# A decoder block on eight cores: prep transfers tied to their moment by semaphores, norm work moved to the front, x loads spread, one weight cast later, elementwise work for two engines

## The chip, the cores and the metric

The kernel runs on one Trainium2 chip, on 8 cores at once. Each core handles one sequence of 4096 tokens, and no core talks to another. The metric is device time in microseconds (us) of the slowest core, lower is better. Some executions fall into a slower state in which the cores of one die (0 to 3 or 4 to 7) or of both are granted a lower TensorE clock. "Fast" below means a run outside that state.

## The reference, cut to what matters

One layer with three sub-layers, each with a conditioned RMSNorm in front, and a final norm:

```python
h = ada_rmsnorm(x, g_ffn1, sh1, sc1)
x = x + 0.5 * gt1 * swiglu_ffn(h, w_ffn1_in, w_ffn1_out)      # d_ff = 2816
h = ada_rmsnorm(x, g_mix, sh2, sc2)
proj = h @ w_in                                                # 1024 -> 2048
y_conv = conformer_conv_group(...)                             # 31-wide conv, LayerNorm, silu
y_rnn  = rglru_group(...)                                      # conv4, gates, linear recurrence
x = x + gt2 * (concat([y_conv, y_rnn]) @ w_out)
h = ada_rmsnorm(x, g_ffn2, sh3, sc3)
x = x + 0.5 * gt3 * swiglu_ffn(h, w_ffn2_in, w_ffn2_out)
return ada_rmsnorm(x, g_final, f_shift, f_scale)
```

Width 1024, float32 in and out. The shifts, scales and gates (`sh1` and so on) come from a small matrix product of the conditioning vector.

## The kernel before

The kernel is written as a list of operations for five queues: PE (TensorE), ACT (ScalarE), DVE (VectorE), SP (SyncE, which issues DMAs) and PL (GpSimd, which issues DMAs that convert float32 to bf16). On the host a list scheduler simulates them and fixes the order of each queue. At any simulated moment, an engine takes the ready operation with the lowest priority number. What the scheduler decides is only an order. At run time the engines are held to each other by semaphores, and only where data or a buffer demands it:

```python
def emit(eng, fn, reads=(), writes=(), dma=None):
    ...
    for r in reads:
        need(r.w)                      # wait for the writer
    for w in writes:
        need(w.w)                      # wait for the last writer and the readers
        ...
```

An operation can also be told to come `after` another. In this kernel that matters to the scheduler alone. No semaphore carries it.

The sequence is cut into 8 tiles of 512 tokens. The first FFN runs over pairs of tiles (4 pairs). The mixer and the second FFN run tile by tile. In the first pair the weights of the first FFN are cast while they are loaded, and written back to DRAM as bf16. All other weights are cast by 54 "prep" transfers, DRAM to DRAM, on GpSimd's queue, each placed `after` a matmul of the pairs 2 to 4:

```python
prep = [(nm, r) for nm in ("win", "dcw", "wout", "w2i", "w2o") for r in range(len(scr[nm]))]
...
for n, (nm, r) in enumerate(prep):
    a = mid[min(len(mid) - 1, n * len(mid) * 9 // (len(prep) * 10))]
    dma("PL", lambda d=d: d.ap, lambda src=src: src, 3 << 19, lambda n=n: psems[n % 8],
        [], [d, psem[n % 8]], after=(a,), prio=450 + n)
```

The norm is a sum of squares (ScalarE squares, TensorE sums over partitions with a matrix of ones), a reciprocal root on ScalarE, then a product on VectorE and a shift on ScalarE, whose bf16 output feeds the matmuls:

```python
def norm(xs, msc, msh, after=()):
    r = stats(xs, after)                       # 8 squares, 8 ones-matmuls, Ln, Exp
    for f in range(8):
        stt(t_, xs[f], gs[msc][:, f], r, ALU.mult, ALU.mult, ...)      # VectorE  (cut)
        act(b, t_, AF.Identity, bias=modv[msh][:, f], ...)             # ScalarE  (cut)
...
for pi, tiles in enumerate(pairs):
    P.prio = 500 + pi * 100
    ...
    hbs = [norm(xs, M_SC1, M_SH1, after=(last_in,)) for xs in xss]
...
def mix_ffn2(t):
    P.prio = 1000 + 10 * t
    ...
    hb = norm(xs, M_SC2, M_SH2)
    ...                                        # mixer of tile t
    P.prio = 1100 + 10 * t
    hb2 = norm(xs, M_SC3, M_SH3)
    ...                                        # second FFN of tile t
```

## Time and profile before

| | before |
|---|---|
| time, median of 3 runs | 2750.63 us |
| TensorE busy | 2403.1 of 2746.4 us |
| TensorE waits for the first FFN's weight slabs | 124.5 us, 3 waits |
| TensorE waits for ScalarE's bf16 outputs (`sb_h`) | 124.1 us, 31 waits |

The page of the kernel before, parts 1 and 2 (busy us, share of the span, instructions; then busy tenths in 40 equal slices of about 69 us, TensorE's granted clock in tenths, and the busy share of the DMA engines):

```profile
PE 2403.1 (87%) x11179; PEld 1121.6 (41%) x11392; DVE 985.2 (36%) x1632; ACT 982.6 (36%) x1538; POOL 114.5 (4%) x221
PE   1999829984799689978998998998999999989796
PEclk9999969997899899989999999999999999999998
DMA  9998894589646964534464554554545545545442
```

TensorE is nearly full except at the start and in three hollows (slices 5 to 6, 9 to 10 and 14), where the DMA line reads 8 or 9.

The table of who waited for whom, TensorE's four largest rows (us in total, times, longest):

```profile
PE ps L418 <- DMA sb_slab<-b_w1i: 124.5, 3, 54.4
PE ps L418 <- ACT sb_h L390: 124.1, 31, 16.2
PE ps L418 <- DVE sb_c L394: 35.4, 7, 10.1
PE ps L418 <- ACT sb_c L390: 23.5, 15, 2.0
```

The timeline of DMA issues around the first hollow, first from GpSimd's queue, then from SyncE's (start, us, queue, out<-in, count):

```profile
297.95 3.91 POOL L425 DMA_DIRECT2D b_win<-win  x8
308.72 0.49 POOL L425 DMA_DIRECT2D b_dcw<-dcw  x1 [6.86 <-DMA b_win<-win]
...
347.85 0.49 POOL L425 DMA_DIRECT2D b_wout<-wout  x1 [4.80 <-DMA b_dcw<-dcw]
...
531.10 0.51 POOL L425 DMA_DIRECT2D b_wout<-wout  x1
```

```profile
306.34 81.47 SPq L425 DMA_DIRECT2D sb_c<-x  x16
387.90 1.19 SPq L425 DMA_DIRECT2D sb_slab<-b_w1i  x2
```

Seventeen prep transfers leave in 50 us, then none of them for 183 us, until the next residual stores unblock the queue. In the middle of the burst SyncE needs 81 us to issue 16 loads of x, and the weight slab for which TensorE waits is the next in its queue. The chain of waits shows that two of the 16 issues take 65 of these 81 us, and what follows (start, us, what):

```profile
315.30 16.83 SPq L425
...
332.94 48.54 SPq L425
...
387.90 11.60 DMA sb_slab<-b_w1i
...
400.55 12.67 PE ps L418 x49
...
413.28 10.74 PE ps L418 x49
```

The first piece of 49 matmuls after the stall takes 12.67 us, later ones 10.74.

In the second half of the kernel there are no large holes, but small ones in every tile. TensorE's timeline in one tile of the mixer stage (start, us, operation, out<-in, shapes, count, and in brackets the idle time before and what ended it):

```profile
2042.93 0.38 PE L418 MATMUL ps<-sb_h,sb_ones 128*128 128x512 bf16 x1
2044.69 1.91 PE L418 MATMUL ps<-sb_ub,sb_slab 128*128 128x256 bf16 x16 [1.38 <-ACT sb_c L390]
2048.62 5.30 PE L418 MATMUL ps<-sb_h,sb_slab 128*128 128x512 bf16 x16 [2.02 <-ACT sb_c L390]
...
2071.00 0.38 PE L418 MATMUL ps<-sb_h,sb_ones 128*128 128x512 bf16 x1
2075.60 4.85 PE L418 MATMUL ps<-sb_h,sb_slab 128*128 128x512 bf16 x11 [4.22 <-DVE sb_c L394]
```

Waits of 1.4, 2.0 and 4.2 us.

### The profile page before, as it was taken

To read this page: it belongs to the slowest core of one execution; us is meant where nothing else is said; L and a number is where in the kernel's file an instruction comes from. 1 tells how busy PE (TensorE), PEld (TensorE's weight loads), DVE (VectorE), ACT (ScalarE), POOL (GpSimd) and SP (SyncE) were. 2 spreads that over 40 slices of the span, in tenths; PEclk is the share of its full clock that TensorE was granted. 3 is DMA by queue.
4 is the path that set the end of the run, shared out by engine and by line. 5 is a ranking of instruction groups with operands and counts; after the bars stand their busy time and mean duration, and the time that the engine had idled before them with its cause. 6 is when DMAs were issued, how large, how long until landed. Compare 5 with 4: busy or idle time off the path is not lost.

```text
span 2746.4 us, 34315 instructions; the slowest of 8 cores (2738.7 to 2746.4 us)
## 1 busy us (share of the span) xinstructions
PE 2403.1 (87%) x11179; PEld 1121.6 (41%) x11392; DVE 985.2 (36%) x1632; ACT 982.6 (36%) x1538; POOL 114.5 (4%) x221
## 2 busy tenths in 40 slices
PE   1999829984799689978998998998999999989796
PEld 0444304432344234444444444444454444444343
DVE  4321303231232323266326345255154263362211
ACT  3211201220120311176337338257266274373312
POOL 0001100010001100100000000000000000000000
PEclk9999969997899899989999999999999999999998
DMA  9998894589646964534464554554545545545442
GB/s 264 190 244 219 136 193 143 146 181 115 214 138 177 135 191 157 191 123 154 123 184 145 181 180 146 179 190 161 192 155 168 183 161 166 180 145 184 154 142 73
DMA packets 130365, 460.32 MB, mean 168 GB/s; under 512 B 16048, under 2 KB 16176, under 8 KB 129328
## 3 DMA queue, kind: packets, MB, share of 16 engines
q1 hardware_dynamic: 113184, 378.15, 42.9%
q0 software_dynamic: 17008, 79.97, 16.8%
q8 instruction: 96, 1.57, 0.2%
q14 instruction: 77, 0.63, 0.1%
HBM read 453.07 MB, written 79.69 MB: 194 GB/s over the span
## 4 chain that ended last, share of the span: by engine, by line
PE 78%; ACT 6%; SPq 6%; DMA 4%; issue 3%; DVE 2%; POOL 0%; DVEq 0%; ACTq 0%; POOLq 0%
PE ps L418 78%; SPq L425 6%; ACT sb_c L390 4%; DMA sb_slab<-b_w1i 3%; ACT sb_h L390 1%; DVE sb_c L394 1%; DMA sb_slab<-wmod 1%; ACT L390 1%; DVE sb_c L398 0%; DMA sb_c<-xmid 0%; DVE sb_slab L474 0%; DVE sb_h L408 0%; POOL y L425 0%; DVEq L111 0%; ACTq L111 0%
## 5 line engine op out<-in xcount | busy, mean ns | idle before, releaser
L418 PE MATMUL ps<-sb_h,sb_slab 128*128 128x512 bf16 x9783 | 2206.8, 385 | 255.5 <-DMA sb_slab<-b_w1i 124.5
L418 PEld LDWEIGHTS ps<-sb_h,sb_slab 128*128 128x128 bf16 x9984 | 985.9, 99 | 1457.8 <-issue 317.3
L390 ACT ACTIVATE sb_c<-ps 128x512 f32<-128x512 f32 x400 | 237.0, 596 | 1076.1 <-PE ps L418 1053.6
L398 DVE TENSOR_TENSOR sb_h<-ps,sb_c 128x512 bf16<-128x512 f32 x352 | 242.8, 691 | 942.5 <-PE ps L418 863.3
L390 ACT ACTIVATE sb_h<-sb_c 128x512 bf16<-128x512 f32 x288 | 172.7, 624 | 337.6 <-DVE sb_c L394 198.8
L394 DVE SCALAR_TENSOR_TENSOR sb_c<-ps,sb_gth,sb_c 128x512 f32<-128x512 f32 x128 | 95.4, 749 | 416.2 <-PE ps L418 412.6
L390 ACT ACT_TABLE_LOAD x95 | 121.9, 1283 | 252.4 <-PE ps L418 246.8
L394 DVE SCALAR_TENSOR_TENSOR sb_c<-sb_c,sb_gs 128x512 f32<-128x512 f32 x256 | 173.2, 745 | 62.7 <-ACT sb_c L390 62.7
L418 PE MATMUL ps<-sb_h,sb_ones 128*128 128x512 bf16 x309 | 98.0, 393 | 57.4 <-ACT sb_h L390 53.5
L474 DVE SCALAR_TENSOR_TENSOR sb_slab<-sb_slab,sb_crow 128x1024 f32<-128x1024 f32 x88 | 107.1, 1217 | 83.0 <-DMA sb_slab<-wmod 81.8
L390 ACT ACTIVATE sb_h<-sb_c,sb_modv 128x512 bf16<-128x512 f32 x192 | 126.4, 716 | 20.9 <-DVE sb_c L394 11.4
L418 PE MATMUL ps<-sb_ub,sb_slab 128*128 128x256 bf16 x1024 | 116.1, 273 | 9.5 <-ACT sb_c L390 9.4
L418 PEld LDWEIGHTS ps<-sb_ub,sb_slab 128*128 128x128 bf16 x1024 | 99.1, 98 | 29.7 <-issue 16.6
L425 POOL DMA_DIRECT2D y<-sb_c x64 | 34.4, 540 | 1542.4 <-ACT sb_c L390 1538.9
L398 DVE TENSOR_TENSOR sb_c<-sb_c 128x512 f32<-128x512 f32 x96 | 61.8, 684 | 42.7 <-ACT sb_c L390 42.7
L394 DVE SCALAR_TENSOR_TENSOR sb_c<-ps,sb_modv,sb_c 128x512 f32<-128x512 f32 x64 | 48.0, 751 | 76.2 <-PE ps L418 70.4
L418 PEld LDWEIGHTS ps<-sb_h,sb_ones 128*128 128x128 bf16 x320 | 31.3, 98 | 104.7 <-issue 77.1
L394 DVE SCALAR_TENSOR_TENSOR sb_c<-sb_ux,sb_vecs,sb_c 128x512 f32<-128x512 f32 x96 | 69.5, 745 | 1.7
L425 POOL DMA_DIRECT2D xmid<-sb_c x64 | 34.8, 544 | 762.0 <-DVE sb_c L394 755.6
L390 ACT ACTIVATE sb_c<-ps,sb_vecs 64x256 f32<-64x256 f32 x128 | 60.3, 484 | 14.9 <-PE ps L418 12.4
L394 DVE SCALAR_TENSOR_TENSOR sb_ub<-sb_c,ps 64x256 bf16<-64x256 f32 x128 | 53.8, 420 | 15.0 <-PE ps L418 11.5
L390 ACT ACTIVATE sb_c<-sb_c,sb_lam 128x512 f32<-128x512 f32 x64 | 49.3, 818 | 0.0
(47 smaller groups left out, 472.1 us busy)
## 6 DMA issues: line engine op xcount, KB each, us to landing
sb_slab<-b_w2i SPq DMA_DIRECT2D x176, 512.0 KB, 3.8
sb_slab<-b_w2o SPq DMA_DIRECT2D x96, 512.0 KB, 3.8
sb_slab<-wmod SPq DMA_DIRECT2D x88, 512.0 KB, 6.9
sb_slab<-b_w1i SPq DMA_DIRECT2D x66, 512.0 KB, 5.3
sb_slab<-b_win SPq DMA_DIRECT2D x64, 512.0 KB, 4.3
sb_slab<-b_dcw SPq DMA_DIRECT2D x64, 512.0 KB, 3.6
sb_slab<-b_w1o SPq DMA_DIRECT2D x36, 512.0 KB, 4.5
sb_c<-x SPq DMA_DIRECT2D x64, 256.0 KB, 26.1
```

The costliest lines, as they stand in the source:

```text
L390: return A("ACT", dur, lambda: (lambda o, i: (lambda h: [h.activation(out=o, in_=i, func=func, bias=bias, scale=scale)]))(out(), in_()), r ...
L394: return A("DVE", dur, lambda: (lambda o, a, b: (lambda h: [h.scalar_tensor_tensor(out=o, in0=a, scalar=scalar, in1=b, op0=op0, op1=op1)]) ...
L398: return A("DVE", dur, lambda: (lambda o, a, b: (lambda h: [h.tensor_tensor(out=o, in0=a, in1=b, op=op)]))(out(), in0(), in1()), reads, wr ...
L418: return [h.matmul(o, lhsT=l, rhs=r, start=(first and i == 0), stop=(last and i == n - 1)) for i, (l, r) in enumerate(pr)]
L425: lambda: (lambda o, i: (lambda h: [h.dma_start(out=o, in_=i)]))(out(), in_()),
L474: return lambda h: [h.scalar_tensor_tensor(out=w, in0=w, scalar=1.0, in1=crow.ap, op0=ALU.mult, op1=ALU.mult, accum_out=o)]
```

## The change

Its intent is to use DMA time evenly and to keep TensorE supplied. The diff, cut to its core (the scheduler's handling of an operation that may run on either of two engines, and formatting, are left out; so is one small edit: the loads of the modulation weights, `wmod`, no longer come `after` a step, only the products that use them do):

```diff
-def emit(eng, fn, reads=(), writes=(), dma=None):
+def emit(eng, fn, reads=(), writes=(), dma=None, toks=()):
+    for tok in toks:
+        need(tok)                       # an explicit wait, beside data and buffers
@@ scheduler: transfers have fixed costs in us, by kind, instead of bytes over 280 GB/s
-DMA_BW = 280.0
+D_CAST, D_SLAB, D_CHUNK, D_PREP = 2.7, 1.65, 0.85, 4.6
-            if op in q.deps:
-                q.ready = max(q.ready, op.end)
+            q.ready = max(q.ready, op.end if op in q.deps else s)
@@ 1. prep waits for its matmul by semaphore; w2o is no longer prepped
-        prep = [... for nm in ("win", "dcw", "wout", "w2i", "w2o") ...]
+        prep = [... for nm in ("win", "dcw", "wout", "w2i") ...]
-            dma("PL", ..., [d, psem[n % 8]], after=(a,), prio=450 + n)
+            dma("PL", ..., [d, psem[n % 8]], sync=(a,), prio=450 + n)
@@ 2. x loads of the next pair: one per FFN step instead of all after the fifth
-                if j == 4:
-                    prev_in = ops[-1]
+                if j >= 3:
+                    next_in.append(ops[-1])
@@ 3. norms get a priority of their own
-            hbs = [norm(xs, M_SC1, M_SH1, after=(last_in,)) for xs in xss]
+            hbs = [norm(xs, M_SC1, M_SH1, after=(last_in,), prio=300) for xs in xss]
-            hb = norm(xs, M_SC2, M_SH2)
+            hb = norm(xs, M_SC2, M_SH2, prio=940)
-            hb2 = norm(xs, M_SC3, M_SH3)
+            hb2 = norm(xs, M_SC3, M_SH3, prio=950)
@@ 4. w2o is cast at its first use, in the first tile's second FFN
-                slabs = [load_slab("w2o", 3 * q + s, False) for s in range(3)]
+                slabs = [load_slab("w2o", 3 * q + s, t == 0) for s in range(3)]
@@ 5. squares, shifts and copies may run on VectorE where it is free first
-                act(lambda q=q: q.ap, lambda f=f: xs[f].ap, AF.Square, [xs[f]], [q], after=after)
+                act(o, i, AF.Square, [xs[f]], [q], after=after, prio=prio, alt=v_sq(o, i))
@@ 6. start: the scale's weights are loaded before x, the shift's after
-        P.prio = -20
+        P.prio = -24
         mods(M_SC1, [None] * 8)
         gs_op(M_SC1, V_G1)
+        P.prio = -20
         mods(M_SH1, [None] * 8)
```

More of the change, by code (lines that the diff above doesn't have):

```diff
@@ L161 @@
     __slots__ = ("eng", "dur", "fn", "reads", "writes", "prio", "tset", "deps", "succ", "ndep", "ready",
-                 "idx", "nbytes", "sem", "slab", "end", "after")
+                 "idx", "nbytes", "sem", "slab", "end", "after", "sync", "tok", "alt", "on")
     def __init__(self):
@@ L174, in __init__, with add @@
         self.prio = 0
-    def add(self, eng, dur, fn, reads=(), writes=(), tset=None, nbytes=0, sem=None, slab=None, after=(), prio=None):
+    def add(self, eng, dur, fn, reads=(), writes=(), tset=None, nbytes=0, sem=None, slab=None, after=(), prio=None, sync=(), alt=None):
         op = Op()
+        op.alt = alt
+        op.sync = [a for a in sync if a is not None]
         op.eng, op.dur, op.fn, op.tset = eng, dur, fn, tset
@@ L195, in add @@
         op.after = [a for a in after if a is not None]
+        op.deps.update(op.sync)
         op.deps.discard(op)
@@ L218, in schedule @@
         b.reset(n)
-    ready = {}
     for op in ops:
@@ L228, in schedule, with enter @@
             d.succ.append(op)
+    def enter(op):
+        ready[op.eng].append((op, op.eng, op.dur, op.tset))
+        if op.alt is not None:
+            ready[op.alt[0]].append((op, op.alt[0], op.alt[1], None))
+    ready = {e: [] for e in ("PE", "ACT", "DVE", "SP", "PL")}
     for op in ops:
         if op.ndep == 0:
-            ready.setdefault(op.eng, []).append(op)
-    et = {e: 0.0 for e in ("PE", "ACT", "DVE", "SP", "PL")}
+            enter(op)
+    et = {e: 0.0 for e in ready}
     table = [None]
@@ L237, in schedule, with start_of @@
     left = len(ops)
-    def start_of(op):
-        t = max(et[op.eng], op.ready)
+    def start_of(op, e):
+        t = max(et[e], op.ready)
         for b in op.writes:
@@ L254, in schedule @@
             cand = None
-            for op in lst:
+            for ent in lst:
+                op = ent[0]
                 if op.slab is not None and order is not None and order[op] != next_slab[0]:
                     continue
-                s = start_of(op)
+                s = start_of(op, e)
                 if s is None:
                     continue
-                sw = 0.0
-                if e == "ACT" and op.tset is not None and table[0] not in op.tset:
-                    sw = SWITCH
+                sw = SWITCH if e == "ACT" and ent[3] is not None and table[0] not in ent[3] else 0.0
                 now = s <= et[e] + 0.03
@@ L266, in schedule @@
                 if cand is None or key < cand[0]:
-                    cand = (key, s, op, sw)
+                    cand = (key, s, ent, sw)
             if cand is not None and (best is None or (cand[1], cand[0]) < (best[0], best[1])):
@@ L270, in schedule @@
         if best is None:
-            stuck = {e: [(o.idx, o.prio, [b.name for b in o.writes if b.pool is not None and b.slot is None]) for o in l[:6]]
+            stuck = {e: [(o[0].idx, o[0].prio, [b.name for b in o[0].writes if b.pool is not None and b.slot is None]) for o in l[:6]]
                      for e, l in ready.items() if l}
             raise RuntimeError(f"stuck with {left} left: {stuck} free {[(p.name, len(p.free)) for p in pools]}")
-        s, _, op, sw = best
-        ready[op.eng].remove(op)
+        s, _, (op, e, dur, tset), sw = best
+        for k in ([op.eng] if op.alt is None else [op.eng, op.alt[0]]):
+            ready[k] = [x for x in ready[k] if x[0] is not op]
+        op.on = e
         ideal = op.slab is not None and order is None
@@ L287, in schedule @@
             next_slab[0] += 1
-        if op.eng == "ACT" and op.tset is not None and table[0] not in op.tset:
-            table[0] = op.tset[0]
+        if e == "ACT" and tset is not None and table[0] not in tset:
+            table[0] = tset[0]
         if op.nbytes:
-            et[op.eng] = s + op.dur
+            et[e] = s + dur
             if ideal:
@@ L294, in schedule @@
             else:
-                c = max(s + op.dur, chan[0]) + op.nbytes / DMA_BW / 1000.0
+                c = max(s + dur, chan[0]) + op.nbytes
                 chan[0] = c
@@ L298, in schedule @@
         else:
-            et[op.eng] = s + sw + op.dur
-            op.end = s + sw + op.dur + SEM_LAT
+            et[e] = s + sw + dur
+            op.end = s + sw + dur + SEM_LAT
         seq.append((s, op))
@@ L312, in schedule @@
             q.ndep -= 1
-            if op in q.deps:
-                q.ready = max(q.ready, op.end)
+            q.ready = max(q.ready, op.end if op in q.deps else s)
             if q.ndep == 0:
-                ready.setdefault(q.eng, []).append(q)
+                enter(q)
         left -= 1
@@ L386, in new, with act, v_ts, v_sq @@
             return VB(pool=pool, name=name)
-        def act(out, in_, func, reads, writes, dur=0.6, bias=0.0, scale=1.0, tset=None, prio=None, after=()):
+        def act(out, in_, func, reads, writes, dur=0.6, bias=0.0, scale=1.0, tset=None, prio=None, after=(), alt=None):
             return A("ACT", dur, lambda: (lambda o, i: (lambda h: [h.activation(out=o, in_=i, func=func, bias=bias, scale=scale)]))(out(), in_()),
-                     reads, writes, tset=tset, prio=prio, after=after)
+                     reads, writes, tset=tset, prio=prio, after=after, alt=alt)
+        def v_ts(out, in0, s1, op0, s2=None, op1=None, dur=0.45):
+            if op1 is None:
+                f = lambda: (lambda o, a: (lambda h: [h.tensor_scalar(out=o, in0=a, scalar1=s1, scalar2=None, op0=op0)]))(out(), in0())
+            else:
+                f = lambda: (lambda o, a: (lambda h: [h.tensor_scalar(out=o, in0=a, scalar1=s1, scalar2=s2, op0=op0, op1=op1)]))(out(), in0())
+            return ("DVE", dur, f)
+        def v_sq(out, in0, dur=0.69):
+            return ("DVE", dur, lambda: (lambda o, a: (lambda h: [h.tensor_tensor(out=o, in0=a, in1=a, op=ALU.mult)]))(out(), in0()))
+        def v_cp(out, in_, dur=0.69):
+            return ("DVE", dur, lambda: (lambda o, i: (lambda h: [h.tensor_copy(out=o, in_=i)]))(out(), in_()))
         def stt(out, in0, scalar, in1, op0, op1, reads, writes, dur=0.75, prio=None, after=()):
@@ L421, in mms, with dma @@
             return A("PE", mm_us(n, cols), f, reads, [bank], prio=prio)
-        def dma(q, out, in_, nbytes, sem, reads, writes, slab=None, after=(), prio=None):
+        def dma(q, out, in_, nbytes, sem, reads, writes, slab=None, after=(), prio=None, sync=()):
             return A(q, 0.06 if q == "SP" else 0.3,
                      lambda: (lambda o, i: (lambda h: [h.dma_start(out=o, in_=i)]))(out(), in_()),
-                     reads, writes, nbytes=nbytes, sem=sem, slab=slab, after=after, prio=prio)
+                     reads, writes, nbytes=nbytes, sem=sem, slab=slab, after=after, prio=prio, sync=sync)
         dr = lambda d, r: d[r * 128:(r + 1) * 128, :]
@@ L437, in load_slab @@
                 src = dr(w_src[nm], r)
-                dma("PL", lambda: b.ap, lambda: src, 1 << 20, slot_sem(b, "PL"), [], [b], slab=True, prio=prio, after=after)
+                dma("PL", lambda: b.ap, lambda: src, D_CAST, slot_sem(b, "PL"), [], [b], slab=True, prio=prio, after=after)
                 d = scr[nm][r]
-                dma("SP", lambda: d.ap, lambda: b.ap, 1 << 19, lambda: wb_sems[b.slot], [b], [d], prio=prio)
+                dma("SP", lambda: d.ap, lambda: b.ap, D_SLAB, lambda: wb_sems[b.slot], [b], [d], prio=prio)
             else:
                 d = scr[nm][r]
-                dma("SP", lambda: b.ap, lambda: d.ap, 1 << 19, slot_sem(b), [d], [b], slab=True, prio=prio, after=after)
+                dma("SP", lambda: b.ap, lambda: d.ap, D_SLAB, slot_sem(b), [d], [b], slab=True, prio=prio, after=after)
             return b
         P.prio = -10
-        dma("SP", lambda: V, lambda: vecs_d[:, :], 86 << 10, lambda: sem_v, [], [vecs], prio=-30)
-        dma("SP", lambda: crow.ap, lambda: crow_d[:, :], 1 << 19, lambda: sem_c, [], [crow], prio=-30)
-        dma("PL", lambda: gates.ap, lambda: gates_d[:, :].rearrange("p (c n) -> p c n", c=8), 1 << 19, lambda: sem_g, [], [gates], prio=5000)
+        dma("SP", lambda: V, lambda: vecs_d[:, :], 0.3, lambda: sem_v, [], [vecs], prio=-30)
+        dma("SP", lambda: crow.ap, lambda: crow_d[:, :], D_SLAB, lambda: sem_c, [], [crow], prio=-30)
+        dma("PL", lambda: gates.ap, lambda: gates_d[:, :].rearrange("p (c n) -> p c n", c=8), 1.0, lambda: sem_g, [], [gates], prio=5000, after=(None,))
         sem_v, sem_c, sem_g = newsem("s_vecs"), newsem("s_crow"), newsem("s_gates")
@@ L467, in mods @@
                 src = dr(wmod_d, m + q)
-                dma("SP", lambda b=b: b.ap.bitcast(F32), lambda s=src: s, 1 << 19, slot_sem(b), [], [b], slab=True,
-                    after=(afters[q],), prio=P.prio)
+                dma("SP", lambda b=b: b.ap.bitcast(F32), lambda s=src: s, D_SLAB, slot_sem(b), [], [b], slab=True,
+                    prio=P.prio)
                 o = modr[m].ap[:, q:q + 1]
@@ L494, in build_program, with load_x @@
         tsc(k_(bah.ap), k_(V[:, V_BA:V_BA + 8]), 0.5, None, ALU.mult, None, [vecs], [bah], dur=0.17)
-        def load_x(src, t, prio=None, after=()):
+        def load_x(src, t, prio=None, after=(None,) * 8):
             xs = []
@@ L501, in load_x, with stats @@
                 d = src[t][f]
-                dma("SP", lambda b=b: b.ap, lambda d=d: d.ap, 1 << 18, slot_sem(b), [d], [b], prio=prio, after=after)
+                dma("SP", lambda b=b: b.ap, lambda d=d: d.ap, D_CHUNK, slot_sem(b), [d], [b], prio=prio, after=(after[f],))
                 xs.append(b)
             return xs
-        def stats(xs, after=()):
+        def stats(xs, after=(), prio=None):
             bank = new(ps, "st")
@@ L510, in stats, with norm @@
                 q = new(p1, "xsq")
-                act(lambda q=q: q.ap, lambda f=f: xs[f].ap, AF.Square, [xs[f]], [q], after=after)
-                mms(bank, [(k_(ones.ap), lambda q=q: q.ap)], [q, ones], first=(f == 0), last=(f == 7))
+                o, i = (lambda q=q: q.ap), (lambda f=f: xs[f].ap)
+                act(o, i, AF.Square, [xs[f]], [q], after=after, prio=prio, alt=v_sq(o, i))
+                mms(bank, [(k_(ones.ap), lambda q=q: q.ap)], [q, ones], first=(f == 0), last=(f == 7), prio=prio)
             r = new(p2, "r")
-            act(lambda: r.ap, lambda: bank.ap, AF.Ln, [bank, cst], [r], bias=eps_ap, scale=1.0 / D, tset=(NLE,))
-            act(lambda: r.ap, lambda: r.ap, AF.Exp, [r], [r], scale=-0.5, tset=(NLE,))
-            return r
-        def norm(xs, msc, msh, after=()):
-            r = stats(xs, after)
+            act(lambda: r.ap, lambda: bank.ap, AF.Ln, [bank, cst], [r], bias=eps_ap, scale=1.0 / D, tset=(NLE,), prio=prio)
+            act(lambda: r.ap, lambda: r.ap, AF.Exp, [r], [r], scale=-0.5, tset=(NLE,), prio=prio)
+            return r
+        def norm(xs, msc, msh, after=(), prio=None):
+            r = stats(xs, after, prio)
             hb = []
@@ L523, in norm @@
                 stt(lambda t_=t_: t_.ap, lambda f=f: xs[f].ap, gs[msc].ap[:, f:f + 1], lambda: r.ap, ALU.mult, ALU.mult,
-                    [xs[f], r, gs[msc]], [t_], after=after)
+                    [xs[f], r, gs[msc]], [t_], after=after, prio=prio)
                 b = new(p1, "hb")
-                act(lambda b=b: b.ap, lambda t_=t_: t_.ap, AF.Identity, [t_, modv[msh]], [b], dur=0.7,
-                    bias=modv[msh].ap[:, f:f + 1])
+                o, i = (lambda b=b: b.ap), (lambda t_=t_: t_.ap)
+                act(o, i, AF.Identity, [t_, modv[msh]], [b], dur=0.7, bias=modv[msh].ap[:, f:f + 1], prio=prio,
+                    alt=v_ts(o, i, modv[msh].ap[:, f:f + 1], ALU.add))
                 hb.append(b)
@@ L570, in build_program @@
         pairs = [list(range(p, min(p + 2, n_tiles))) for p in range(0, n_tiles, 2)]
-        prep = [(nm, r) for nm in ("win", "dcw", "wout", "w2i", "w2o") for r in range(len(scr[nm]))]
+        prep = [(nm, r) for nm in ("win", "dcw", "wout", "w2i") for r in range(len(scr[nm]))]
         late = [M_SC2, M_SH2, M_GT2, M_SC3, M_SH3, M_GT3, M_SCF, M_SHF]
@@ L575, in build_program @@
         pair_last = None
-        prev_in = last_in = None
+        prev_in, last_in = [None] * 16, None
         for pi, tiles in enumerate(pairs):
@@ L579, in build_program @@
             lp = -25 if pi == 0 else 400 + pi * 100
-            xss = [load_x(x_dr, t, prio=(-25 if t == 0 else -15) if pi == 0 else lp, after=(prev_in,)) for t in tiles]
-            hbs = [norm(xs, M_SC1, M_SH1, after=(last_in,)) for xs in xss]
+            xss = [load_x(x_dr, t, prio=(-22 if t == 0 else -15) if pi == 0 else lp, after=prev_in[8 * (t % 2):8 * (t % 2) + 8]) for t in tiles]
+            hbs = [norm(xs, M_SC1, M_SH1, after=(last_in,), prio=300) for xs in xss]
             hids = [[] for _ in tiles]
+            next_in = []
             for j in range(FC):
@@ L588, in build_program @@
                     gt_anchor = ops[-1]
-                if j == 4:
-                    prev_in = ops[-1]
+                if j >= 3:
+                    next_in.append(ops[-1])
+            prev_in = next_in
             last_in = ops[-1]
@@ L601, in build_program @@
                         b, d = xs[fc], xm_dr[t][fc]
-                        dma("PL", lambda d=d: d.ap, lambda b=b: b.ap, 1 << 18, slot_sem(b, "PL"), [b], [d])
+                        dma("PL", lambda d=d: d.ap, lambda b=b: b.ap, D_CHUNK, slot_sem(b, "PL"), [b], [d])
         first_mid = next(k for k, (pi, _) in enumerate(anchors) if pi == min(1, len(pairs) - 1))
@@ L612, in build_program @@
             src, d = dr(w_src[nm], r), scr[nm][r]
-            dma("PL", lambda d=d: d.ap, lambda src=src: src, 3 << 19, lambda n=n: psems[n % 8], [], [d, psem[n % 8]], after=(a,),
+            dma("PL", lambda d=d: d.ap, lambda src=src: src, D_PREP, lambda n=n: psems[n % 8], [], [d, psem[n % 8]], sync=(a,),
                 prio=450 + n)
@@ L631, in mix_ffn2 @@
             gate_op = (last_in, anchors[-1][1])[t] if t < 2 else ffn_anchor[t - 2]
-            xs = load_x(xm_dr, t, after=(gate_op,))
-            hb = norm(xs, M_SC2, M_SH2)
+            xs = load_x(xm_dr, t, after=(gate_op,) * 8)
+            hb = norm(xs, M_SC2, M_SH2, prio=940)
             def w256(slab, kc, o):
@@ L644, in mix_ffn2 @@
                     mms(bank, [(w256(slab, kc, 128 * e), lambda kc=kc: hb[kc].ap) for kc in range(8)], [slab] + hb)
-                    act(lambda c=c: ux[c].ap[:, 3:3 + T], lambda bank=bank: bank.ap, AF.Copy, [bank], [ux[c]])
+                    o, i = (lambda c=c: ux[c].ap[:, 3:3 + T]), (lambda bank=bank: bank.ap)
+                    act(o, i, AF.Copy, [bank], [ux[c]], alt=v_cp(o, i))
                     b = new(p2, "xr")
@@ L707, in mix_ffn2 @@
                     for q in range(2):
-                        act(lambda v=v, hh=hh, q=q: v.ap[64 * hh:64 * hh + 64, q::2],
-                            lambda bank=bank, hh=hh, q=q: bank.ap[64 * q:64 * q + 64, 256 * hh:256 * hh + 256], AF.Identity,
-                            [bank, vecs], [v], dur=0.45, bias=V[64 * q:64 * q + 64, V_CONVB + g:V_CONVB + g + 1], scale=0.5)
+                        o = lambda v=v, hh=hh, q=q: v.ap[64 * hh:64 * hh + 64, q::2]
+                        i = lambda bank=bank, hh=hh, q=q: bank.ap[64 * q:64 * q + 64, 256 * hh:256 * hh + 256]
+                        cb = V[64 * q:64 * q + 64, V_CONVB + g:V_CONVB + g + 1]
+                        act(o, i, AF.Identity, [bank, vecs], [v], dur=0.45, bias=cb, scale=0.5,
+                            alt=v_ts(o, i, 0.5, ALU.mult, cb, ALU.add, dur=0.42))
                 cv.append(v)
@@ L717, in mix_ffn2 @@
                 cp(lambda b=b: b.ap, lambda c=c: cv[c].ap, [cv[c]], [b])
-                act(lambda q=q: q.ap, lambda c=c: cv[c].ap, AF.Square, [cv[c]], [q])
+                o, i = (lambda q=q: q.ap), (lambda c=c: cv[c].ap)
+                act(o, i, AF.Square, [cv[c]], [q], alt=v_sq(o, i))
                 mms(bm, [(k_(ones.ap), lambda b=b: b.ap)], [b, ones], first=(c == 0), last=(c == 3))
@@ L769, in mix_ffn2 @@
                 stt(lambda b=b: b.ap, lambda b=b: b.ap, gs[M_SCF].ap[:, f:f + 1], lambda r=r: r.ap, ALU.mult, ALU.mult, [r, gs[M_SCF]], [b])
-                act(lambda b=b: b.ap, lambda b=b: b.ap, AF.Identity, [modv[M_SHF]], [b], dur=0.7, bias=modv[M_SHF].ap[:, f:f + 1])
+                o = lambda b=b: b.ap
+                act(o, o, AF.Identity, [modv[M_SHF]], [b], dur=0.7, bias=modv[M_SHF].ap[:, f:f + 1],
+                    alt=v_ts(o, o, modv[M_SHF].ap[:, f:f + 1], ALU.add))
                 d = VB(ap=dr(y_d, t * 8 + f))
-                dma("PL", lambda d=d: d.ap, lambda b=b: b.ap, 1 << 18, slot_sem(b, "PL"), [b], [d])
+                dma("PL", lambda d=d: d.ap, lambda b=b: b.ap, D_CHUNK, slot_sem(b, "PL"), [b], [d])
         for t in range(n_tiles):
@@ L791, in emit_cb @@
         def emit_cb(op):
-            fn = op.fn()
+            fn = (op.fn if op.on == op.eng else op.alt[2])()
             rs = [b.res for b in op.reads]
             ws = [b.res for b in op.writes]
-            e = engs[op.eng]
+            e = engs[op.on]
+            toks = [a.tok for a in op.sync]
             if op.nbytes:
                 sm = op.sem()
-                emit(e, fn, rs, ws, dma=sm)
+                op.tok = emit(e, fn, rs, ws, dma=sm, toks=toks)
                 stores[sm] = sm.val
             else:
-                emit(e, fn, rs, ws)
+                op.tok = emit(e, fn, rs, ws, toks=toks)
         seq, end = schedule(P, pools, sl, order, emit_cb)
```

## The prediction

> **What bounds the kernel now.** The page's busy table gives TensorE 2403 of 2746 us (87%), VectorE and ScalarE 36% each. In the chain of waits a piece of 49 matmuls takes 10.74 us, 219 ns per 512 columns; I count 10,880 (1,360 per 512-token tile): an estimated floor near 2385 us. So some 340 us are TensorE idle time. TensorE waits (table of waits): 124.5 us for the first FFN's weight slabs (54.4, 50.4, 19.8), 124.1 us for ScalarE's normalised activations (56.5 at the start, about 9.6 at each of three pair boundaries, 15.2 before the last tile's second FFN), 35.4 us for VectorE, 23.5 us for other ScalarE results.
>
> **Why the slabs are late.** The timeline of DMA issues shows the 54 weight-prep transfers (float32 to bf16, DRAM to DRAM, GpSimd's queue) in three bursts, at 298-352, 597-648 and 894-928 us: no semaphore holds them to the planned moment. One follows another by about 4.7 us. In the first burst SyncE needs 81 us (306-388) to issue the next pair's 16 x loads, and the slab that TensorE needs stands behind them; DMA share there is 0.96. The Trainium skill, "DMA: Bandwidth & Descriptors", section "Issuing engines are not separate DMA queues", says all issuing engines feed the same 16 DMA engines; this trace agrees.
>
> **What the change does, with my costs.**
> 1. Prep waits for its matmul anchor: 42 transfers, one per about 18 us. x loads go out one per FFN step. Estimated DMA demand per pair 183 of 285 us. Saves nearly all of 124.5 us, plus about 2 us of slow clock after each stall (12.67 against 10.74 us for 49 matmuls): -128.
> 2. Norm statistics first: the three pair boundaries (-27), the last tile's wait (-15). The wait before the first mixer tile (10.2) may stay: its priority still follows the last FFN pair's.
> 3. Two-engine choice: VectorE copies of about 0.42-0.69 us for ScalarE's 0.60-0.72. Neither engine is full; it helps in the mixer, where TensorE waits about 8 us per tile: -2 us per tile, and 10 of the 33 us in the first mixer tile: -24 in all.
> 4. Start: scale weights before x, shift after: -4 of 56.5.
> 5. w2o cast at first use: 12 prep transfers fewer, but 12 casts and write-backs inside the first tile's second FFN, whose output part lasts about 38 us; the first pair's casts took a median 19.5 us to land. With ten slabs of lead: +8 (0 to 25).
> 6. Imperfect pacing: +5.
>
> Sum -186: 2564 us. Nearly all of 1, 2 and 4 is on the critical path, since TensorE has nothing to run there.
>
> **Prediction: 2564 us**, 8 in 10 between 2525 and 2625. Faster by over 2%: 0.94; within 2%: 0.03; slower: 0.03.
>
> **What would show it.** Prep issues spread over 300-1000 us; waits for the first FFN's slabs below 15 us; no 81 us stretch of x issues; waits for normalised activations 65-80 us, mostly the start; granted clock near 1.0 from the third slice to the sixteenth; at most a small new wait on w2o slabs.
>
> **What would make it wrong.** GpSimd's queue is in order: a waiting prep transfer holds back residual stores behind it, and with them buffers and x loads. Casts of w2o, whose write-backs SyncE must wait for in order, could stall the next tile's loads by more than 25 us. More work on VectorE could delay PSUM evictions. The mixer's serial chain may not shorten.

## The result, and the profile after

The ratios in this document are the mean time of one kernel's fast runs over the mean of the other's fast runs of the same rounds.

The changed kernel takes 2485.3 to 2488.2 us in its three fast runs, mean 2486.8. The ratio to the kernel before is 0.9037 (95% interval 0.902 to 0.9055). The prediction was 2564 us, with a range from 2525: the direction was right, and the gain was 264 us where 186 were forecast. It lies outside the range.

The page of the changed kernel, the same lines:

```profile
PE 2361.1 (95%) x11177; PEld 1114.5 (45%) x11392; DVE 1057.8 (43%) x1795; ACT 911.9 (37%) x1382; POOL 115.2 (5%) x221
PE   1999999999999999899899999999999999999996
PEclk9999999999999999899999999999999999999998
DMA  9899489669856764554966555555555545555451
```

TensorE's four largest rows in the table of waits:

```profile
PE ps L443 <- ACT sb_h L401: 75.4, 17, 15.8
PE ps L443 <- DVE sb_h L413: 6.5, 3, 3.3
PE ps L443 <- ACT sb_c L401: 4.7, 6, 2.0
PE ps L443 <- DVE sb_c L409: 3.3, 5, 0.7
```

The hollows are gone, and so are the waits for the first FFN's slabs. But the row of 35.4 us for VectorE is gone as well, and the 23.5 us for ScalarE has shrunk to 4.7. Those are the small waits in the mixer tiles that the prediction left standing for the most part. GpSimd's queue now issues one prep transfer per 7 to 14 us, with pauses of up to 45 us around the residual stores (42 of them from 314 to 887 us, one per 14 us on average where the prediction said about 18):

```profile
314.20 0.51 POOL L450 DMA_DIRECT2D b_win<-win  x1 [3.80 <-PE ps L443]
321.10 0.50 POOL L450 DMA_DIRECT2D b_win<-win  x1 [6.39 <-PE ps L443]
334.89 0.49 POOL L450 DMA_DIRECT2D b_win<-win  x1 [13.29 <-PE ps L443]
```

Where the 263 us of the two traces came from can be read at three milestones: the last residual store (end of the first FFN), the last store of the first tile's output, and the last store of the sixth tile's.

| stage | before | after | difference |
|---|---|---|---|
| to the last residual store | 1160 | 999 | -161 |
| from there to the first tile's output | 374 | 340 | -33 |
| five further tiles | 956 | 919 | -36 |
| last two tiles, to the end | 257 | 225 | -32 |

The prediction had about -154 (terms 1, 2 without the last tile, 4 and 6) for the first line. For the other three together it had about -31 (the last tile's wait, the mixer, w2o). They brought -102. The five tiles after the change are not alike: the second tile, in whose stretch the w2o casts fall, takes 202 us, the other four 178 to 180. So an ordinary tile went from 191 to about 180 us.

### The profile page after: what moved, and what is told of

Read it like the earlier page. It is cut to its first block, busy times and chain, and to the rows that moved or that the text cites. A ratio compares the mean times of both kernels' runs of the same rounds, so it can differ in the third digit from the quotient of the medians.

```text
span 2483.8 us, 34258 instructions; the slowest of 8 cores (2468.5 to 2483.8 us)
## 1 busy us (share of the span) xinstructions
PE 2361.1 (95%) x11177; PEld 1114.5 (45%) x11392; DVE 1057.8 (43%) x1795; ACT 911.9 (37%) x1382; POOL 115.2 (5%) x221
## 4 chain that ended last, share of the span: by engine, by line
PE 90%; DMA 5%; ACT 2%; issue 1%; SPq 1%; DVE 1%; POOL 0%; DVEq 0%; POOLq 0%; ACTq 0%
PE ps L443 90%; DMA sb_slab<-wmod 2%; DMA sb_c<-x 1%; SPq L450 1%; DMA sb_c<-xmid 1%; ACT sb_c L401 1%; DMA sb_slab<-w2o 1%; ACT sb_h L401 1%; DVE sb_c L419 0%; DVE sb_c L409 0%; DVE sb_slab L499 0%; DVE sb_ub L419 0%; ACT L401 0%; POOL y L450 0%; DVEq L113 0%
## 5 line engine op out<-in xcount | busy, mean ns | idle before, releaser
L443 PE MATMUL ps<-sb_h,sb_slab 128*128 128x512 bf16 x9776 | 2182.2, 380 | 28.7 <-ACT sb_h L401 15.8
L401 ACT ACTIVATE sb_h<-sb_c 128x512 bf16<-128x512 f32 x241 | 148.9, 628 | 387.2 <-DVE sb_c L419 234.4
L443 PE MATMUL ps<-sb_h,sb_ones 128*128 128x512 bf16 x313 | 106.6, 394 | 67.0 <-ACT sb_h L401 59.6
L401 ACT ACTIVATE sb_h<-sb_c,sb_modv 128x512 bf16<-128x512 f32 x162 | 107.4, 719 | 15.6 <-DVE sb_modv L423 8.8
L401 ACT ACTIVATE sb_c<-sb_c 128x512 f32<-128x512 f32 x72 | 44.0, 626 | 2.2
```

The lines of the kernel that those rows point to most:

```text
L401: return A("ACT", dur, lambda: (lambda o, i: (lambda h: [h.activation(out=o, in_=i, func=func, bias=bias, scale=scale)]))(out(), in_()), r ...
L443: return [h.matmul(o, lhsT=l, rhs=r, start=(first and i == 0), stop=(last and i == n - 1)) for i, (l, r) in enumerate(pr)]
```

## The experiments

Twelve kernels. The kernel before ran beside each call (mean of its fast runs 2747.6, 2753.4 and 2755.4 us), so ratios are compared across calls, and differences in us are ratio differences times 2750. All kernels gave correct results. Names that begin with `a_` are the changed kernel with something undone, `b_` the kernel before with something added.

| kernel | fast runs | mean of them, us | ratio to before |
|---|---|---|---|
| changed kernel | 3 | 2486.8 | 0.9037 |
| a_nosync | 2 | 2578.0 | 0.9383 |
| b_sync | 3 | 2624.2 | 0.9552 |
| a_noprio | 4 | 2576.7 | 0.9379 |
| a_noalt | 2 | 2487.9 | no interval |
| b_sync_prio | 4 | 2488.7 | 0.9039 |
| a_noprio_noalt | 3 | 2611.0 | 0.9486 |
| a_w2oprep | 4 | 2475.0 | 0.8989 |
| a_xburst | 3 | 2480.5 | 0.9009 |
| b_sync_p950 | 3 | 2517.1 | 0.9138 |
| b_sync_p300 | 3 | 2597.0 | 0.9425 |
| b_sync_p940 | 2 | 2598.9 | 0.9432 |
| best1 | 3 | 2480.3 | 0.9001 |

One remark on b_sync: one of its three fast runs (2646.6 us) had the second die at clocks of 0.947 to 0.968. Its two undisturbed runs are 2612.5 and 2613.7 us. In the third run the first die's cores took 2607.6 to 2610.1 us, as in these two. I use the mean of the two, 2613.1, which is 0.951 of the kernel before.

### The theories

The first-FFN part behaved nearly as predicted, so the question is the mixer stage. Theory A: the norms' priorities did it. With the second FFN's norm done early, TensorE has FFN matmuls at hand while the mixer's chain of small operations runs. Theory B, the one the prediction used: the choice of two engines shortened that chain. Beside it stands the question whether pacing alone or the spread x loads removed the hollows.

### a_nosync: the semaphore taken off again

```diff
-            dma("PL", ..., [d, psem[n % 8]], sync=(a,), prio=450 + n)
+            dma("PL", ..., [d, psem[n % 8]], after=(a,), prio=450 + n)
```

The order of instructions on all five engines is the same as in the changed kernel. Only the waits differ.

> The changed kernel with one thing undone: the 42 prep transfers keep their place in the queue's order but no longer wait for their matmul anchor on a semaphore. The instruction order on all five engines is identical to the changed kernel's, only the waits differ. Pacing theory: the three bursts come back, TensorE waits again for the first FFN's slabs, 80 to 130 us in all (the prediction put 124.5 + 6 us on it), so 2565 to 2615 us against 2486. Rival (spreading the x loads was enough, since in the kernel before the needed slab stood behind 16 x loads): below 2510 us.

Measured: ratio 0.9383, 95 us more than the changed kernel (2573.8 and 2582.2 us). The waits are back (the table of waits of this run):

```profile
PE ps L443 <- DMA sb_slab<-b_w1i: 86.2, 5, 35.4
```

The longest is 35 us instead of 54, with five waits instead of three, while the x loads are still spread and w2o still not prepped. So the spread alone does not remove the hollows, and the semaphore does.

### b_sync: the semaphore alone

The kernel before with `sync` in place of `after` for its 54 prep transfers. The host's simulation sees `sync` too, so the order is not quite the old one: in a rebuild, 12 of the 217 places in GpSimd's queue and 116 of TensorE's 1600 hold another operation. a_nosync is the cleaner test, and the two agree.

> The kernel before with one thing added: prep transfers wait for their anchor by semaphore; x loads still in one burst per pair, priorities, engines and the w2o prep as before. If pacing alone is worth what the prediction gave it: 2751 - 128 = about 2623 us, waits for the first FFN's slabs below 15 us, the three boundary waits of about 9.6 us still there. If pacing needs the spread x loads or the new cost model of the transfers, less than half of it: above 2690 us.

Measured: 2613.1 us undisturbed, 135 us less than before; 128 for this term was the prediction. The row for slabs is gone from the table of waits, and the last residual store comes at 1026 instead of 1160 us. The three waits at pair boundaries (9.7, 8.2 and 8.2 us) remain. The mixer tiles take the same 191 us as before. Pacing works alone, and what it gains lies in the first FFN alone (134 us before the last residual store).

### a_noprio and a_noalt: the two theories for the mixer

```diff
 a_noprio
-            hbs = [norm(xs, M_SC1, M_SH1, after=(last_in,), prio=300) for xs in xss]
+            hbs = [norm(xs, M_SC1, M_SH1, after=(last_in,)) for xs in xss]
-            hb = norm(xs, M_SC2, M_SH2, prio=940)
+            hb = norm(xs, M_SC2, M_SH2)
-            hb2 = norm(xs, M_SC3, M_SH3, prio=950)
+            hb2 = norm(xs, M_SC3, M_SH3)
 a_noalt
-        op.alt = alt
+        op.alt = None
```

> The changed kernel with the norms' priorities undone (first FFN, mixer and second FFN norms back at their tile's own priority). The prediction missed about 80 us in the mixer stages: there a tile now takes 179.5 us instead of 191. Priority theory: the early norm of the second FFN gives TensorE matmuls to fill the mixer's serial chain, so without it the tiles go back to about 188 to 191 us, the waits at the pair boundaries and before the last tile return: 2570 to 2600 us. Rival (the two-engine choice shortened the chain, as the prediction had it): below 2530 us, tiles still near 180 us.

> The changed kernel without the choice of engine: every elementwise op back on ScalarE. Rival theory (two engines shorten the mixer): tiles at 188 us or more, 2540 us or more. Priority theory: the mixer's chain is hidden anyway, 2490 to 2505 us, ScalarE's busy time back at about 983 us with little effect.

Measured: without the priorities 2576.7 us (ratio 0.9379, 94 us lost). Without the engine choice 2487.7 and 2488.1 us in its two fast runs, 1 us from the changed kernel (there is no interval, and by the ratio to its own kernel before, 2487.9 / 2747.6 = 0.9055, the loss would be 5 us). Theory B falls as an explanation of the miss. ScalarE's busy time rose from 912 to 1039 us in that run with almost no effect on the time. (Both figures lie outside what I had expected, 2490 to 2505 us and about 983 us.)

The waits at the pair boundaries (9.6 us each) and before the last tile (15.0 us) returned, as expected. The five tiles take 939 us, 188 each, but not evenly: the outputs come in alternating gaps of about 157 and 208 us, which I had not expected and cannot explain. Without the priorities the changed kernel is already a little better in the mixer than the kernel before (956). The next run says why.

### a_noprio_noalt: both undone

> The changed kernel with both the norms' priorities and the two-engine choice undone. Undone alone, they cost 90 us and about 1 us. If the engine choice is worth nothing at all: 2577 us, as without the priorities alone. If it is a second way to the same gap (worth something only while the mixer's chain is exposed): 2595 to 2620 us, tiles back at 191 us as in the kernel before.

Measured: 2611.0 us, ratio 0.9486, 29 us worse than without the priorities alone; the five tiles take 960 us, 192 each, again unevenly. So the engine choice is worth some 29 us while the mixer's chain is exposed (in the two traces 21 of it in the five tiles, 4 per tile where the prediction had 2, and 5 in the first tile's stage where it had 10, so that the nearness to the predicted 24 us is partly luck), and next to nothing (1 to 5 us) once the priorities have covered the chain. The two are rival remedies for one gap, and the sum in the prediction counted the weaker one.

### b_sync_prio: the two strong parts, and nothing else

The kernel before plus the semaphore plus the three priorities: no spread x loads, w2o prepped, one engine per operation, the old cost model.

> The kernel before with two things added: the semaphore pacing (measured alone: 2612 us fast against 2748) and the norms' priorities. If these two are the whole gain: 2612 - 90 to - 125, so 2487 to 2525 us, tiles of the mixer stage at about 180 us instead of 191. If the priorities need the two-engine choice, the new cost model or the spread x loads to work: above 2560 us.

Measured: 2488.7 us, ratio 0.9039 (0.9023 to 0.9054), the same as the full change. Two edits give the whole gain.

### b_sync_p300, b_sync_p940, b_sync_p950: which norm

Pacing plus one of the three priorities each.

> Kernel before + pacing, with the priority only for the norm of the second FFN. Theory (this norm stood behind the next tile's mixer work on VectorE and ScalarE, so that TensorE ran out of matmuls in the mixer): nearly all of the mixer-stage gain comes from it: tiles at 180 to 183 us instead of 191, no 15 us wait before the last tile, the three boundary waits of 8 to 10 us stay: 2505 to 2530 us.

> Kernel before + pacing, with the priority only for the norms of the first FFN. It should only remove the three boundary waits (8.2 to 9.7 us each, and some slow clock after each): 25 to 32 us less than pacing alone, 2580 to 2590 us; tiles of the mixer stage still at 191 us.

> Kernel before + pacing, with the priority only for the norm of the mixer. What is left over for it by difference is small: 2600 to 2615 us, tiles near 190 us. If it is this norm, not the second FFN's, that fills the gaps: below 2570 us.

Measured against pacing alone (0.951): the second FFN's norm 0.9138, 102 us; the first FFN's 0.9425, 23 us; the mixer's 0.9432, 21 us. Together they are 0.9039, 130 us; the single gains sum to about 146, so they may overlap a little (each ratio is known to about 0.002 or 0.003, which is 6 to 8 us). Two expectations were missed by a little: b_sync_p300 (2596 to 2598 us) gained less than the 25 to 32 us, b_sync_p940 (2598.7 and 2599.1) more than expected. The traces place b_sync_p940's gain before the first tile's output (359 us from the last residual store, against 376 with pacing alone): the wait of 10.2 us before the first mixer tile, which the prediction let stand, is gone. Both keep tiles of 191 us. Only b_sync_p950 changes the tiles: five take 900 us, 180 each, where pacing alone and the other two take 956. In its trace the three boundary waits stay (8 to 10 us each) and the 15 us wait before the last tile is gone, as expected.

The busy time in one and the same stretch, 1600 to 2160 us, of pacing alone and then of pacing with that one priority (length, TensorE busy and its matmuls, weight loads, VectorE, ScalarE, GpSimd, granted clock, DMA share, GB/s):

```profile
1600.00:2160.00 560.00, 535.37 (x2604) 255.87 (x2603) 242.28 (x409) 289.19 (x444) 8.61 (x16) 0.98 0.55 170
```

```profile
1600.00:2160.00 560.00, 557.15 (x2758) 268.52 (x2757) 252.16 (x426) 306.28 (x468) 12.93 (x24) 1.00 0.59 181
```

In 560 us TensorE does 2758 matmuls instead of 2604. Its waits in the stretch, pacing alone:

```profile
PE ps L422 <- DVE sb_c L398: 12.7, 3, 4.2
PE ps L422 <- ACT sb_c L394: 10.2, 6, 2.0
```

With the small rows these are 24.5 us, and with the priority 2.6 us:

```profile
PE ps L422 <- ACT sb_h L394: 1.7, 6, 0.4
PE ps L422 <- ACT sb_c L394: 0.9, 3, 0.4
```

The stretch holds about three tiles (560 / 191), so the waits are about 8 us per tile, as the prediction counted. A tile got 11 us shorter all the same. The rest is the clock: 0.98 instead of 1.00 over 560 us is 11 us, or nearly 4 per tile. The clock is printed to two digits only, but the timeline of the kernel before, with the same waits, says the same: 1.8 us lost by the 16 matmuls after the second wait, 2.4 by the 11 after the third.

Why this norm? The timeline of pacing alone, VectorE, ScalarE and TensorE at the end of a tile's mixer (1931 to 1945 us). Rows `sb_c<-sb_c,sb_gs` are the norm's products on VectorE, `sb_h<-sb_c,sb_modv` its shifts on ScalarE, `sb_h<-sb_c,sb_vecs` the silu at the end of the mixer's convolution branch:

```profile
1931.38 1.41 DVE L398 SCALAR_TENSOR_TENSOR sb_c<-sb_c,sb_gs 128x512 f32<-128x512 f32 x2 [0.24 <-ACT sb_c L394]
...
1938.72 2.49 DVE L402 TENSOR_TENSOR sb_c<-sb_c 128x512 f32<-128x512 f32 x4
1938.88 0.71 ACT L394 ACTIVATE sb_h<-sb_c,sb_modv 128x512 bf16<-128x512 f32 x1
1939.48 0.38 PE L422 MATMUL ps<-sb_h,sb_ones 128*128 128x512 bf16 x1
...
1940.90 2.93 ACT L394 ACTIVATE sb_h<-sb_c,sb_vecs 128x512 bf16<-128x512 f32 x4
...
1941.79 3.39 DVE L398 SCALAR_TENSOR_TENSOR sb_c<-sb_c,sb_gs 128x512 f32<-128x512 f32 x5
1944.09 15.66 PE L422 MATMUL ps<-sb_h,sb_slab 128*128 128x512 bf16 x64 [4.23 <-DVE sb_c L398]
1944.26 3.77 ACT L394 ACTIVATE sb_h<-sb_c,sb_modv 128x512 bf16<-128x512 f32 x6
```

A norm of eight pieces is squeezed in between the mixer's last operations, and its shifts are done only at 1948 us. TensorE stops at about 1939.9 us and starts again at 1944.09, and what it then gets are 64 matmuls, the output projection's number (8 times 8). The silu (1940.90 to 1943.83) had just ended; the profile names VectorE, but with several semaphores waited for it can only name the latest by its own clock. There was nothing else to run: the next FFN's input was one of the things still in the making. With the priority, the shifts of a tile period lie in two compact blocks outside the mixer's chain, and FFN matmuls run beside it (ScalarE and TensorE of b_sync_p950, one period):

```profile
1825.27 5.36 ACT L394 ACTIVATE sb_h<-sb_c,sb_modv 128x512 bf16<-128x512 f32 x8 [1.02 <-DVE sb_c L398]
...
1890.48 2.93 ACT L394 ACTIVATE sb_h<-sb_c,sb_vecs 128x512 bf16<-128x512 f32 x4
1893.84 6.21 PE L422 MATMUL ps<-sb_h,sb_slab 128*128 128x512 bf16 x28
...
1921.58 5.00 ACT L394 ACTIVATE sb_h<-sb_c,sb_modv 128x512 bf16<-128x512 f32 x8
```

The trace does not say to which tile a row belongs; that the squeezed norm is the second FFN's is read from the code and from the fact that moving this norm alone removes the gap. The order that the host plans agrees: in a rebuild of b_sync the eight products of the second FFN's norm of one tile stand in VectorE's queue among the last operations of the next tile's mixer, first two, then one, then five together, as the trace has them.

### a_w2oprep, a_xburst and best1: the two remaining parts, and a better version

```diff
 a_w2oprep
-        prep = [... for nm in ("win", "dcw", "wout", "w2i") ...]
+        prep = [... for nm in ("win", "dcw", "wout", "w2i", "w2o") ...]
-                slabs = [load_slab("w2o", 3 * q + s, t == 0) for s in range(3)]
+                slabs = [load_slab("w2o", 3 * q + s, False) for s in range(3)]
 a_xburst
-                if j >= 3:
-                    next_in.append(ops[-1])
+                if j == 4:
+                    next_in = [ops[-1]] * 16
 best1: both
```

> The changed kernel with w2o back among the paced prep transfers (54 instead of 42, one per 14 us) and loaded as bf16 in the first tile too. The prediction charged the cast at first use with +8 us (the trace of the changed kernel shows a wait of 9.4 us there); if pacing has room, undoing it gives 2472 to 2482 us and no wait there. If the denser prep hurts the first FFN: 2490 us or more, with waits for its slabs.

> The changed kernel with all 16 x loads of a pair issued together again after the fifth FFN step, on the same order of all other engines. With paced prep the transfers have room, so I expect no difference from 2486 us beyond 5 us. If the spread was needed: waits for the first FFN's slabs reappear, 20 us or more. It might even win a few us: x loads of the second pair then come before the write-backs behind which they now stand (a wait of 5 us).

> The changed kernel with w2o back among the paced prep transfers and the x loads issued together again. Measured alone against the changed kernel's 2486: -12 and -5 us. If they add: 2467 to 2472 us; if both remove the same wait: about 2474.

Measured: with w2o prepped 2475.0 us (ratio 0.8989 against 0.9037: 13 us better than the change; the intervals, up to 0.9004 and from 0.902, do not overlap). The cast at first use costs what its chain of waits in the changed kernel shows:

```profile
1207.86 14.94 DMA sb_slab<-w2o
...
1223.37 12.38 DMA sb_c<-xmid
...
1236.60 10.23 PE ps L443 x34
```

SyncE must wait for a cast to land before it can issue the write-back, and behind that write-back in the same queue stood the loads of a later tile's residual. TensorE waited 9.4 us, though not on a w2o slab.

With the x loads in one burst 2480.5 us, ratio 0.9009, 8 us better, though the intervals (0.8991 to 0.9027 and 0.902 to 0.9055) overlap. That is a little outside the 5 us within which I expected no difference. The wait of 5 us at the second pair is gone, because the loads no longer stand behind the write-backs of the first pair.

Both together gave 2480.3 us, more than either expectation: the gains do not add. (By the ratios, 0.9001 and 0.8989, it is 3 us behind a_w2oprep, within the noise.) In this run waits for the first FFN's slabs appear (8.9 us in 2 waits), which neither kernel alone shows. All 54 transfers and the burst are not enough for such waits: b_sync, b_sync_p940 and b_sync_p950 have both and show none. They appear in the three runs that also have the priority of the first FFN's norm (b_sync_p300 10.3 us, b_sync_prio 7.6, best1 8.9), and not in a_w2oprep, which has that priority and 54 transfers but spreads the x loads. So in these runs the spread is of use only where the other two come together. The lowest time found is a_w2oprep's, 2473.8 to 2477.8 us in four fast runs.

## Why the prediction was wrong

Each term of its sum, as the prediction put it, and what the runs showed:

| term | predicted | measured |
|---|---|---|
| 1. prep paced, x loads spread | -128 | pacing alone -135 (b_sync); the spread itself +8 (a_xburst) |
| 2. norm statistics first | -42 | -130 on top of pacing (b_sync_prio); of these b_sync_p950 alone -102 |
| 3. two-engine choice | -24 | -1 to -5 beside the priorities (a_noalt), -29 without them (a_noprio_noalt) |
| 4. start | -4 | 0: the first long run of matmuls begins at 65.8 instead of 66.0 us |
| 5. w2o cast at first use | +8 | +13 (a_w2oprep) |
| 6. imperfect pacing | +5 | not separable; no slab wait is left |

**Right.** The diagnosis of the hollows, their price and their cure (term 1). The boundary waits of term 2: b_sync_p300 gained 23 us where 27 were expected for them. The direction and nearly the size of term 5; the danger named at the prediction's end, write-backs that hold SyncE's queue, is what the chain shows. The signs that were to show it came too: waits for ScalarE's `sb_h` of 75.4 us (65 to 80 expected), no slab waits (under 15), and prep issues from 314 to 887 us.

**The step that failed** is in terms 2 and 3: "it helps in the mixer, where TensorE waits about 8 us per tile: -2 us per tile". The prediction gave the norms' priorities only the waits that the table ascribes to `sb_h` at the boundaries and before the last tile, and took the small waits inside a tile for the mixer's own latency, which only faster elementwise work could shorten. Two things were wrong with that:

1. *Whose wait it is.* The table names what ended a wait. It does not name what could have run instead. In these tiles the mixer's chain ended the wait, but TensorE had nothing else to do because another tile's norm stood behind that chain in the order of VectorE and ScalarE. Moving this one norm forward removed nearly all of the 8 us per tile (24.5 to 2.6 us in 560 us). The engine choice without the priorities took the same waits only from 19.5 to 13.3 us (a_noprio_noalt, a_noprio).
2. *What a wait costs.* The prediction charged about 2 us of slow clock to each of the three long stalls, but nothing to the small ones. They cost nearly 4 us per tile more. The Trainium skill, "TensorE: Matmul & The Clock Gate", section "What's actually happening", says that TensorE falls to half rate after an idle window of about 3.4 us and needs as long of work to return; the trace shows the effect after the small waits too (5.30 us for 16 matmuls that take 3.5; granted clock 0.69 from 2050 to 2055 us and, after the wait of 4.2 us, 0.50 from 2075 to 2080). So a tile shrank by 11 us and not by 2.

The first tile's output also came 33 us sooner; 10 was allowed for that stage in term 3, less 8 for w2o. In b_sync_p950 that stage takes 345 us against 376 with pacing alone, so the same norm alone can bring this gain; the mixer's norm alone brings 17 us of it (b_sync_p940), so the two overlap here.

**What stays open.** The full change equals b_sync_prio (0.9037 and 0.9039), although it also carries the cast of w2o (+13) and the spread x loads (+8). So something else in it gives about 20 us back. The traces place nearly all of it at the end: from the sixth output to the last store the changed kernel takes 215 us (2259 to 2474), b_sync_prio 233 (2242 to 2475). a_noalt takes 227 there (one trace of each), so 12 of the 18 us go with the engine choice; in a_noalt they are made up for before the second tile's output, which comes 12 us earlier than in the changed kernel (1530 against 1542). That is why a_noalt as a whole is only 1 to 5 us slower. The other 6 us may be the new costs and start times in the scheduler's model, the `wmod` loads or the order at the start; no run separates these. The other thing open is why best1's waits appear (54 transfers, the burst and the first FFN's norm early): that these three compete for the DMA engines is argued, not measured by itself.

## What to carry to other kernels

A planned order is not a planned time: a queue of transfers with nothing to wait for runs as early as its queue lets it, and a burst can then stand in front of the one load that matters; a semaphore on the intended moment cured that alone. In a software pipeline like this one, give the producers of the filler work (here the norm in front of the next block of matmuls) a higher rank than the latency-bound chain that they are meant to cover. When a wait is small but comes with every tile, ask what else the engine could have run, and count the slow clock that follows; then do not add up remedies that close the same gap.

## What the Trainium skill lacked or had wrong

- "DMA: Bandwidth & Descriptors", section "Issuing engines are not separate DMA queues", says that the time to initiate a DMA "is usually small relative to the DMA itself". Under the prep burst 16 issues of 256 KB loads took 81.47 us on SyncE, two of them 16.83 and 48.54 us, while the same queue's issue of a w2o slab took 0.32 us in the quiet part. What can hold an issue on this chip is not said on that page, and no run here shows it either; the trace shows that the DMA engines were busy all the time (share 0.99 from 306 to 388 us) and moved only 122 GB/s, against 339 GB/s at a share of 0.97 just after (399.7 to 405 us).
- "TensorE: Matmul & The Clock Gate", section "What's actually happening", gives a window of about 3.4 us of idle time as what sends the clock down. Here two waits of 1.38 and 2.02 us with 1.9 us of work between them were followed by 16 matmuls in 5.30 us instead of 3.5, so shorter gaps can do it; whether the second alone would have is not shown. The page does say further on that frequent short idle times bring the clock down; what it lacks is their length. After a long stall the trace is near the page: 12.67 - 10.74 = 1.9 us lost, as at half rate for 3.9 us.
